# Down projections of a two-layer decoder: 20 of 43 blocks of K in Strassen quads with seven products for eight

## The chip, the core and the metric

The kernel runs on one core of a Trainium2 chip. The metric is the device time of one launch in microseconds. TensorE (PE) multiplies, with its weight loads (PEld) beside it; VectorE (DVE) and ScalarE (ACT) compute elementwise; GpSimd (POOL) and SyncE (SP) issue transfers here, and POOL does little else.

## The reference, cut to what matters

Two decoder layers on 256 tokens of width 2048. Layer 0 attends with 16 full heads, layer 1 with 16 query heads on 4 key-value heads, a sliding window and sinks. After each attention and each gated mixer the residual is normalised.

```
h = layer_norm(ALPHA * h + attn, ...)
ffn:  h @ w_up -> causal width-3 conv -> g, v = split;  (gelu(g) * v) @ w_down
h = layer_norm(ALPHA * h + ffn, ...)
```

`w_up` is 2048 x 11008, `w_down` 5504 x 2048 (43 blocks of 128 rows of K, four column chunks of 512). Everything is in float32.

## The kernel before

Every product of a float32 activation and a float32 weight is made of three matmuls in the format fp32r. Each operand is split in two: a rounded high part, by ScalarE's Copy, and a low part, the difference, by VectorE. A product is high x high, high x low and low x high. The weights come from one long stream in DRAM, `wst`, in the order of their use, in *halves* of 128 x 1024 floats (512 KB). `load_weights` (L75, issued by SP) brings a half into one of four `raw` buffers; `high_upto` (L94, ScalarE) and `low_piece` (L103, VectorE) split it into one of four pairs `wh`, `wl`. `take` asks for the half three ahead of the one that PE starts (`AHEAD`). When the low part of half s is made, its raw buffer is free and the load of half s+4 is issued. All engines run their instructions in the order in which the program records them; small work is recorded through an agenda: `at(n, f)` records `f` n slots later, where each half of the stream is one slot.

In the *up projection* (`ws_unit`, L244 and L246) the weights are stationary, a unit takes two halves, and VectorE does the convolution (L639 to L642), the gate (L645) and the split of the gated result (`store`, L650) into 43 blocks of `st` and `up`, where columns 0 to 255 are the high part of 256 tokens and columns 256 to 511 the low part.

In the *down projection* (`project_out`, with the class `Moving`, L307 to L309) the activations are stationary and 512 columns of weights move. A half holds two blocks of K for one chunk of 512 columns, and each block serves both token tiles: 12 matmuls a half. There are 43 x 4 blocks, so 86 halves a layer. Two PSUM banks hold a chunk; after it, `evac` adds them to the scaled residual `res` and takes the statistics (L380, L381). The last eight halves of the last chunk are the *window*: PE goes through them once for token tile 0 and a second time for tile 1, so that VectorE normalises tile 0 (L396, L397) and PE transposes it (L406) for the next stage during the second pass. The window's halves stay in places of their own (`aside`): in layer 0 in `xT` and in `st`. `settle` lets the splits run ahead there, in a ring of free places (`reach`), up to six halves into the next layer; VectorE has them all in order ahead of the evacuation of tile 0. Layer 1's end has only four places in `xT` and no ring.

`gb` holds the scale and bias of the norm (two transfers of 1 MB on POOL); `banks` of PSUM are four "acc" and four "at" tiles, and the down projection uses "acc" alone until its transposes.

Of the kernel before, what the change touches and what calls it, by code (L numbers as in the profile page):

```python
# [11 lines left out]
F32 = mybir.dt.float32  # L12
F32R = mybir.dt.float32r
AF = mybir.ActivationFunctionType
ALU = mybir.AluOpType
# [21 lines left out]
RAW_BUFS = 4  # L37
# [8 lines left out]
OPENING = 4  # L46


@with_exitstack
def trunk(ctx: ExitStack, tc: tile.TileContext, wst, xT_in, x_in, relb, onehot, umask, sinks, conv_in, ln_g, ln_b, out):  # L50
# [9 lines left out]
    gbp = ctx.enter_context(tc.tile_pool(name="gbp", bufs=1))  # L60

    n_halves = wst.shape[0]
# [7 lines left out]
    def load_weights(behind=None):  # L70
        u = todo["load"]
        if u < n_halves:
            raws[u] = wpool.tile([P, HW], F32, name="raw")
            for j, c in enumerate(pieces(u)):
                nc.sync.dma_start(raws[u][:, c], wst[u][:, c])  # L75
                if behind:
                    behind(j)
            todo["load"] += 1
# [70 lines left out]
    st = big.tile([P, NH, 2 * T], F32R, name="st")  # L149

# [197 lines left out]
    def project_out(src, nk, li, homes, preload, turnover=None):  # L348
# [4 lines left out]
        mv = Moving(src, nk)  # L353
        w0 = nexth["i"] + (nk * NCH - WINDOW_BLOCKS) // 2
        n0 = w0 + WINDOW
        after = homes is not None
        aside.update({w0 + j: (xT, j) for j in range(SPARE)})

        def settle():


            ring, h = homes()
            aside.update({w0 - len(ring) + j: x for j, x in enumerate(ring) if x})
            aside.update({w0 + SPARE + j: h[j] for j in range(4)})
            aside.update({n0 + 4: h[4], n0 + 5: h[5], n0 + 6: h[0], n0 + 7: h[1]})
# [8 lines left out]
        for i, a in enumerate((ln_g, ln_b)):  # L374
# [3 lines left out]
        def evac(n, t, acc):  # L378
            z = res[:, t, n * 512:(n + 1) * 512]
            nc.vector.scalar_tensor_tensor(z, z, ALPHA, acc, op0=ALU.mult, op1=ALU.add)  # L380
            nc.vector.bn_stats(stats[:, t, n, :], z)  # L381
# [33 lines left out]

        def late(t, i):
            last = i == WINDOW - 1
            if t == 0 and last:
                evac(NCH - 1, 0, accs[0])
                sd = moments(0)  # L420
                nc.vector.reciprocal(rs[0], sd)
                for c in COLS[0]:
                    norm(0, c)
            if t == 1 and after:
                if 3 <= i < 7:
                    c = COLS[0][i - 3]
                    low(0, c, turn(0, c))
                if 5 <= i < 7:
                    high_upto(n0 + i + 1)
            if t == 1 and last:  # L430
                evac(NCH - 1, 1, accs[1])
# [6 lines left out]
        for n in range(NCH):  # L438
            accs = [acc_tile(), acc_tile()]
            if n == 1 and turnover:  # L440
                turnover()
            if n == 1 and after:
                settle()
            if n < NCH - 1:
                mv.chunk(accs)
                for t in range(2):
                    at(0, evac, n, t, accs[t])
            else:
                nc.scalar.activation(junk, eps, AF.Sqrt)
                mv.chunk(accs, late=late)  # L450
# [65 lines left out]
    def layer_attention(l, rest, stage, turnover):  # L516
# [62 lines left out]

        if l == 0:  # L580
# [14 lines left out]
        return project_out(lambda k: oT[:, k, :], NH, 2 * l, turnover.homes, AF.Gelu_apprx_tanh, turnover)  # L595

    class FeedForward:
# [12 lines left out]
        def homes(self):  # L610
            x, h = ([(tile, j) for j in range(n)] for tile, n in ((xT, SPARE), (self.up, 6)))
            return x + h[:4] + HALF_BUFS * [None] + h[4:], h

        def block(self, k):
            return st[:, k, :] if k < NH else self.up[:, k - NH, :]

        def run(self, rest):
# [29 lines left out]
            def store(i, g):  # L647
                b = self.block(i)
# [22 lines left out]
            ws_opening(accs, between, opened)  # L671
            for u in range(OPENING, 2 * FT):
                acc = acc_tile()
                ws_unit(acc)
                after(u, acc)
            homes = None
            if l == 0:
                x, h = ([(tile, j) for j in range(n)] for tile, n in ((xT, SPARE), (st, 4)))
                homes = lambda: (x + HALF_BUFS * [None], h + [(self.up, j) for j in range(2)])
            return project_out(self.block, FT, 2 * l + 1, homes, AF.Exp)  # L680
# [41 lines left out]

def _stream(w_qkv, w_o0, w_kv, w_q, w_o1, w_up, w_down):
# [7 lines left out]
    def ffn(l):  # L731
        up = w_up[l]
        parts.append(np.stack([_still(up[:, :DFF]), _still(up[:, DFF:])], 1).reshape(-1, P, HW))
        parts.append(_moving(w_down[l]))
# [45 lines left out]
```

## Time and profile before

| what | value |
| --- | --- |
| median of 3 runs | 2093.8 us (2093.42 to 2095.63) |
| span of the profiled execution | 2091.8 us |
| TensorE busy | 2074.2 us (99%) |
| VectorE busy | 1439.6 us (69%) |
| ScalarE busy | 968.7 us (46%) |
| moved by the DMA engines | 405 MB, 194 GB/s in the mean |
| granted TensorE clock, mean | 0.998 |

For the profiled execution the span is given, from its first to its last instruction; it is 2.0 us under the median of the runs. In a row of a view by lines, the numbers after the bar are the busy time of the group, the mean length of one instruction in ns, and the idle time of the engine ahead of them with what ended it. In a timeline row, the first number is the start, the second the length, both in us; "[1.66 <-PE acc L309]" says that the engine stood idle for 1.66 us until that instruction was done. A matmul's length contains its passage through the array: the pace is read from the starts.

### The profile page before, as it was taken

The numbers are of one execution on the slowest core, as the hardware profiler recorded it, in microseconds if no ns is written. First come the engines' busy times: TensorE is split into PE (matmuls) and PEld (weight loads), VectorE is DVE, ScalarE is ACT, GpSimd is POOL, SyncE is SP. The second block draws the span as 40 slices with busy tenths as digits, with TensorE's granted clock in tenths as the row PEclk, the third lists the DMA queues.
The fourth block names the chain that finished last, engine by engine and source line by source line (L and its number), as shares of the span: only waits on it lengthen the run. The fifth ranks groups of instructions, "written<-read, shape, count | busy, mean of one in ns | idle before, by whom it ended". The sixth has DMA issues, their size and how long they took to land.

```text
span 2091.8 us, 28873 instructions
## 1 busy us (share of the span) xinstructions
PE 2074.2 (99%) x11076; PEld 1792.3 (86%) x11076; DVE 1439.6 (69%) x2106; ACT 968.7 (46%) x1397; POOL 23.5 (1%) x36
## 2 busy tenths in 40 slices
PE   9999999999999999999999999999999999999997
PEld 7888888988888888888888888898888888888886
DVE  5555567787877788744466676778778778765545
ACT  5444445344444454433353555444444454443342
POOL 0100000000000000000000000000000000000000
PEclk9999999999999999999999999999999999999999
DMA  8855557455555565655573745645556565566653
GB/s 273 305 167 180 166 181 253 161 173 191 185 192 188 190 189 185 205 197 192 191 261 125 248 149 186 232 152 191 182 195 188 186 194 185 191 202 196 195 192 131
DMA packets 114264, 405.09 MB, mean 194 GB/s; under 512 B 15648, under 2 KB 15968, under 8 KB 112848
## 3 DMA queue, kind: packets, MB, share of 16 engines
q1 hardware_dynamic: 106832, 383.67, 56.5%
q0 software_dynamic: 7008, 19.33, 2.6%
q8 instruction: 87, 1.43, 0.3%
q14 instruction: 49, 0.40, 0.1%
q10 hardware_dynamic: 288, 0.26, 0.1%
HBM read 401.02 MB, written 6.34 MB: 195 GB/s over the span
## 4 chain that ended last, share of the span: by engine, by line
PE 95%; DMA 2%; DVE 2%; ACT 1%; issue 0%; SPq 0%; ACTq 0%; DVEq 0%
PE acc L244 36%; PE acc L246 19%; PE acc L307 12%; PE acc L308 12%; PE acc L309 12%; DMA raw<-in_wst_dram 2%; PE acc L271 1%; PE at L499 1%; PE at L466 1%; ACT wh L94 1%; PE at L406 1%; DVE wl L103 0%; PE at L492 0%; PE at L465 0%; PE at L500 0%
## 5 line engine op out<-in xcount | busy, mean ns | idle before, releaser
L103 DVE TENSOR_TENSOR wl<-raw,wh 128x1024 fp32r<-128x1024 f32 (+1 forms) x663 | 790.8, 1220 | 303.8 <-ACT wh L94 297.9
L244 PE MATMUL acc<-xT,wh 128*128 128x512 f32 x3456 | 832.7, 392 | 0.0
L94 ACT ACTIVATE wh<-raw 128x1024 fp32r<-128x1024 f32 (+1 forms) x663 | 676.0, 1053 | 329.7 <-PE acc L309 272.2
L244 PEld LDWEIGHTS acc<-xT,wh 128*128 128x128 f32 x3456 | 641.1, 188 | 128.5
L246 PEld LDWEIGHTS acc<-xT,wl 128*128 128x128 f32 x3456 | 444.1, 190 | 14.9 <-DVE wl L103 2.4
L246 PE MATMUL acc<-xT,wl 128*128 128x256 f32 x3456 | 453.1, 284 | 1.8 <-DVE wl L103 1.8
L638 ACT ACTIVATE h<-acc 128x256 f32<-128x256 f32 x172 | 66.3, 385 | 411.3 <-PE acc L246 216.0
L639 DVE TENSOR_TENSOR h<-acc,h 128x256 f32<-128x256 f32 x172 | 73.0, 424 | 157.1 <-ACT h L638 157.1
L307 PE MATMUL acc<-wh,up 128*128 128x512 f32 x378 | 147.0, 389 | 0.0
L308 PE MATMUL acc<-wl,up 128*128 128x512 f32 x378 | 147.0, 389 | 0.0
L309 PE MATMUL acc<-wh,up 128*128 128x512 f32 x378 | 147.0, 389 | 0.0
L307 PE MATMUL acc<-wh,st 128*128 128x512 f32 x366 | 143.7, 393 | 0.0
L308 PE MATMUL acc<-wl,st 128*128 128x512 f32 x366 | 142.5, 389 | 0.0
L309 PE MATMUL acc<-wh,st 128*128 128x512 f32 x366 | 142.5, 389 | 0.0
L641 DVE SCALAR_TENSOR_TENSOR c<-h,cw,c 128x255 f32<-128x255 f32 x172 | 83.3, 484 | 6.1
L642 DVE SCALAR_TENSOR_TENSOR c<-h,cw,c 128x254 f32<-128x254 f32 x172 | 83.2, 484 | 6.2
L307 PEld LDWEIGHTS acc<-wh,up 128*128 128x128 f32 x378 | 70.9, 188 | 14.8
L309 PEld LDWEIGHTS acc<-wh,up 128*128 128x128 f32 x378 | 70.9, 188 | 14.8
L308 PEld LDWEIGHTS acc<-wl,up 128*128 128x128 f32 x378 | 71.0, 188 | 14.6
L309 PEld LDWEIGHTS acc<-wh,st 128*128 128x128 f32 x366 | 68.7, 188 | 14.5
L307 PEld LDWEIGHTS acc<-wh,st 128*128 128x128 f32 x366 | 68.7, 188 | 14.0
L308 PEld LDWEIGHTS acc<-wl,st 128*128 128x128 f32 x366 | 68.7, 188 | 13.9
(129 smaller groups left out, 1636.8 us busy)
## 6 DMA issues: line engine op xcount, KB each, us to landing
raw<-in_wst_dram SPq DMA_DIRECT2D x723, 512.0 KB, 4.2
band<-ud POOLq DMA_DIRECT2D x8, 512.0 KB, 13.4
bias<-band POOLq DMA_DIRECT2D x8, 512.0 KB, 6.3
gb<-in_ln_g_dram POOLq DMA_DIRECT2D x4, 1024.0 KB, 7.0
gb<-in_ln_b_dram POOLq DMA_DIRECT2D x4, 1024.0 KB, 10.1
res<-in_x_dram POOLq DMA_DIRECT2D x2, 1024.0 KB, 10.5
out_dram<-res SPq DMA_DIRECT2D x8, 256.0 KB, 2.5
xc<-in_xT_dram SPq DMA_DIRECT2D x7, 256.0 KB, 5.6
```

The source lines that it names most:

```text
L94: nc.scalar.activation(wh[:, c], raws[s][:, c], AF.Copy)
L103: nc.vector.tensor_tensor(out=wl[:, c], in0=raws[s][:, c], in1=wh[:, c].bitcast(F32), op=ALU.subtract)
L244: nc.tensor.matmul(acc, w, xT[:, k, :], start=(k == 0), stop=(k == ends[0]))
L246: nc.tensor.matmul(acc[:, 0:T], w, xT[:, k, 0:T], start=False, stop=(k == ends[1]))
L271: nc.tensor.matmul(part(accs[u]), cols(pair[u][k // 8][0], k % 8), part(xT[:, k, :]), start=(t == 0 and k == 0), stop=False)
L307: nc.tensor.matmul(acc, sh, wh, start=(k == 0), stop=False)
L308: nc.tensor.matmul(acc, sh, wl, start=False, stop=False)
L309: nc.tensor.matmul(acc, sl, wh, start=False, stop=(k == self.nk - 1))
L638: nc.scalar.activation(h, acc[:, T:2 * T], AF.Copy)
L639: nc.vector.tensor_tensor(out=h, in0=acc[:, 0:T], in1=h, op=ALU.add)
L641: nc.vector.scalar_tensor_tensor(c[:, 1:T], h[:, 0:T - 1], w[:, 1:2], c[:, 1:T], op0=ALU.mult, op1=ALU.add)
L642: nc.vector.scalar_tensor_tensor(c[:, 2:T], h[:, 0:T - 2], w[:, 0:1], c[:, 2:T], op0=ALU.mult, op1=ALU.add)
```

## The change

**Quads.** The first 20 blocks of K are taken as 10 quads: two blocks of K (k1, k2) by two token tiles (0, 1), times a pair of column chunks (n0, n1). The eight block products of a quad become seven (Winograd's form of Strassen), each of three matmuls: B11 and B21 with the blocks themselves, and five with a sum or difference on one side or both. Of the weights, `T1`, `T3`, `T2`, `T4` stand for sums and differences of B11, B12, B21, B22; of the activations, s1, s2, s4 are sums, and the difference of k1's two token tiles stands in the place of k1's second tile, written at the gate (`store`, for even i below 20). Two quads are a *run* of seven halves, in which a block of weights serves one product: 6 matmuls a half. The other 23 blocks stay plain, and their halves stand around the runs by `PLAINS`. The two column pairs have 58 halves each, 116 a layer for 86. All eight PSUM banks are used: four "acc", and four "at" for the sums P1, P5, P6, P7, which `fold` later adds to the residual.

**Weights.** The host puts B11, B12, B22, B21 of each quad into a second array `wsum`. `presums` loads them (two transfers of 512 KB on SP), lets VectorE form the four sums (1024 + 512 + 512 columns) and stores them to DRAM by POOL (1 MB), once for each of 20 quads and layer: four under attention, 16 in the up projection, one every nine slots. The runs load T halves from there. The buffer for it is the one of `gb`, so the down projection's two transfers into `gb` move to slots 54 and 103 of its 116.

**Activations.** `sums` and `split_sums` make s1, s2, s4 of two quads into `xT`, five times a layer, at the end of the run before.

**Rest.** The raw buffers become five. The places of layer 0's window are put in another order, since `st` and `xT` are read by quads until later. The scratch for DMA descriptors is set to 4096.

```diff
-RAW_BUFS = 4
+RAW_BUFS = 5
+NQ = 10
+PLAINS = ((5, 4, 3, 3, 3, 5), (2, 2, 2, 2, 2, 13))
+EARLY = 4
+SEVEN = (("B11", "B21"), ("T1", "T3"), ("T2", "T4"), ("B22", "B22"), ("B11", "B21"), ("T1", "T3"), ("T2", "T4"))
...
+    def presums(quads, first_slot, pitch):
+        area = gbp.tile([P, 2, D], F32, name="gb")
+        r, w = area[:, 0], area[:, 1]
+        def load(q, j):
+            js = slice(j * HW, (j + 1) * HW)
+            nc.sync.dma_start(r[:, js], wsum[q][:, js])
+        def first():
+            nc.vector.tensor_tensor(out=w[:, 0:HW], in0=r[:, 512:512 + HW], in1=r[:, 0:HW], op=ALU.subtract)
+        def second(q):
+            nc.vector.tensor_tensor(out=w[:, HW:HW + 512], in0=r[:, 0:512], in1=w[:, 512:HW], op=ALU.add)
+            nc.vector.tensor_tensor(out=w[:, HW + 512:], in0=r[:, HW + 512:], in1=w[:, HW:HW + 512], op=ALU.subtract)
+            nc.gpsimd.dma_start(wsums[q], w)
+        for i, q in enumerate(quads):
+            m = first_slot + pitch * i
+            at(m, load, q, 0)
+            at(m + 1, load, q, 1)
+            at(m + 5, first)
+            at(m + 6, second, q)
...
+            return [{"B11": (("P1", n), *token(k1, 0)), "B21": ((n0, 0), *token(k2, 0)), "T1": (("P5", n), *s1),
+                     "T3": (("P7", n), *token(k1, 1)), "T2": (("P6", n), *s2), "T4": ((n0, 1), *token(k2, 1)),
+                     "B22": ((n1, 0), *s4)}[b]]
...
+        def fold(c):
...
+            def first():
+                nc.scalar.activation(u, p1, AF.Copy)
+                into(0, n0, u)
+                nc.vector.tensor_tensor(out=u, in0=p6, in1=u, op=ALU.add)
+                nc.vector.tensor_tensor(out=v, in0=p5, in1=u, op=ALU.add)
+            def second():
+                into(0, n1, v)
+                nc.vector.tensor_tensor(out=u, in0=p7, in1=u, op=ALU.add)
+            def third():
+                into(1, n0, u)
+                into(1, n1, u)
+                into(1, n1, p5)
+            for i, f in enumerate((first, second, third)):
+                at(1 + i, f)
+        def sums(i):
...
+            nc.vector.tensor_tensor(out=g.rearrange("p (a b) -> p a b", a=4), in0=x[:, :, 0:T].bitcast(F32),
+                                    in1=x[:, :, T:2 * T].bitcast(F32), op=ALU.add)
...
+            for o, a, b, op in ((s2, gv[:, :, 1, 1], gv[:, :, 0, 1], ALU.subtract), (s1, s2, gv[:, :, 0, 0], ALU.add),
+                                (s4, gv[:, :, 1, 0], s2, ALU.subtract)):
+                nc.vector.tensor_tensor(out=o, in0=a, in1=b, op=op)
...
+        def split_sums(i, s):
+            hi, lo = (xsum(i)[:, h].rearrange("p s q c -> p (s q c)") for h in range(2))
+            nc.scalar.activation(hi, s, AF.Copy)
+            nc.vector.tensor_tensor(out=lo, in0=s, in1=hi.bitcast(F32), op=ALU.subtract)
...
+        if quads:
+            for i in range(NQ // 2):
+                at(1 + (i and sum(PLAINS[0][:i]) + 7 * (i - 1) + 2), all_sums, i)
...
+        presums([(l, *q) for q in QUAD_ORDER[:EARLY]], 4 if l else 40, 9)
...
             def store(i, g):
+                if i < 2 * NQ and i % 2 == 0:
+                    nc.vector.tensor_tensor(out=g[:, P:T], in0=g[:, 0:P], in1=g[:, P:T], op=ALU.subtract)
...
+            presums([(l, *q) for q in QUAD_ORDER[EARLY:]], 0, 9)
...
-    nc = _bacc.Bacc("TRN2", target_bir_lowering=False, num_devices=1)
+    nc = _bacc.Bacc("TRN2", target_bir_lowering=False, num_devices=1, dynamic_dma_scratch_size=4096)
```

On TensorE, before, in layer 0's down projection: two blocks of one half (`wh_8064`, `wl_8065`), each for both token tiles (banks `acc_8114` and `acc_8115`).

```order
L307 MATMUL acc_8114<-wh_8064,st_82 128x512
L308 MATMUL acc_8114<-wl_8065,st_82 128x512
L309 MATMUL acc_8114<-wh_8064,st_82 128x512
L307 MATMUL acc_8115<-wh_8064,st_82 128x512
L308 MATMUL acc_8115<-wl_8065,st_82 128x512
L309 MATMUL acc_8115<-wh_8064,st_82 128x512
```

Now, the end of the first run there: the T2 and T4 blocks of its last half (`wh_8444`, `wl_8445`), then the plain half behind it (`wh_8463`, `wl_8464`).

```order
L509 MATMUL at_8437<-wh_8444,xT_123 128x512
L510 MATMUL at_8437<-wl_8445,xT_123 128x512
L511 MATMUL at_8437<-wh_8444,xT_123 128x512
L509 MATMUL acc_8312<-wh_8444,st_125 128x512
L510 MATMUL acc_8312<-wl_8445,st_125 128x512
L511 MATMUL acc_8312<-wh_8444,st_125 128x512
L509 MATMUL acc_8308<-wh_8463,up_2986 128x512
L510 MATMUL acc_8308<-wl_8464,up_2986 128x512
```

Each block of the run has three matmuls for six, one product into one bank; the sums of activations come from `xT`.

On VectorE, at the same place, now: the splits of the run's last two halves (`wl_8432`, `wl_8445`), the sums of the next two quads, the split of the plain half, the low part of the sums. Before, splits alone stand in a row here.

```order
L168 TENSOR_TENSOR wl_8432<-raw_8352,wh_8431 128x1024
L168 TENSOR_TENSOR wl_8445<-raw_8372,wh_8444 128x1024
L564 TENSOR_TENSOR tmp_8450<-st_125 128x1024
L570 TENSOR_TENSOR tmp_8451<-tmp_8450 128x256
L570 TENSOR_TENSOR tmp_8451<-tmp_8451,tmp_8450 128x256
L570 TENSOR_TENSOR tmp_8451<-tmp_8450,tmp_8451 128x256
L168 TENSOR_TENSOR wl_8464<-raw_8390,wh_8463 128x1024
L576 TENSOR_TENSOR xT_123<-tmp_8451,xT_123 128x768
```

Four operations moved in between the split of the run's last half and that of the half behind it.

On VectorE at the end of layer 0's down projection, before: splits into `wl`, `xT`, `st` and `up` (the last six belong to the next layer), then the evacuation of tile 0.

```order
L103 TENSOR_TENSOR xT<-raw,xT 128x1024 x4
L103 TENSOR_TENSOR st<-raw,st 128x1024 x4
L103 TENSOR_TENSOR wl<-raw,wh 128x1024 x4
L103 TENSOR_TENSOR up<-raw,up 128x1024 x2
L380 SCALAR_TENSOR_TENSOR res<-res,acc 128x512
```

Now, from the splits of the window's fourth half on:

```order
L168 TENSOR_TENSOR st<-raw,st 128x1024 x2
L527 SCALAR_TENSOR_TENSOR res<-res,tmp 128x512
L550 TENSOR_TENSOR tmp<-at,tmp 128x512
L525 TENSOR_TENSOR res<-res,acc 128x512
L531 BN_STATS stats<-res 128x6
L527 SCALAR_TENSOR_TENSOR res<-res,acc 128x512
L168 TENSOR_TENSOR xT<-raw,xT 128x1024 x2
L525 TENSOR_TENSOR res<-res,tmp 128x512
L531 BN_STATS stats<-res 128x6
L527 SCALAR_TENSOR_TENSOR res<-res,tmp 128x512
L525 TENSOR_TENSOR res<-res,at 128x512
L168 TENSOR_TENSOR st<-raw,st 128x1024
```

Two parts of the fold (its first part, three operations, stands two splits and more ahead) and an evacuation moved in among the window's splits; behind these rows come the same six splits for the next layer and the evacuation of tile 0.

More of the change, by code (lines that the diff above doesn't have):

```diff
@@ L373, in project_out, with load_gb @@
         gb = gbp.tile([P, 2, D], F32, name="gb")
-        for i, a in enumerate((ln_g, ln_b)):
+        def load_gb(i):
+            a = (ln_g, ln_b)[i]
             nc.gpsimd.dma_start(gb[:, i], bass.AP(tensor=a.tensor, offset=a.offset + li * D, ap=[[0, P], [1, D]]))
-        ag, rs = {}, {}
[L378 to L381, printed above, removed]
+        whole = sum(PLAINS[0]) + 7 * (NQ // 2)
@@ new lines, in project_out, with product @@
+        for half in plan:
+            for e in half:
+                for key, _, _ in target(e):
+                    owed[key] = owed.get(key, 0) + 1
+        def product(key, sh, sl, wh, wl):
+            if key not in banks:
+                banks[key] = psum.tile([P, 512], F32, name="at" if key[0] in SUMS else "acc")
+                used[key] = 0
+            acc, first, last = banks[key], used[key] == 0, used[key] == owed[key] - 1
+            used[key] += 1
+            nc.tensor.matmul(acc, sh, wh, start=first, stop=False)
+            nc.tensor.matmul(acc, sh, wl, start=False, stop=False)
+            nc.tensor.matmul(acc, sl, wh, start=False, stop=last)
@@ new lines, in done, with zs, into @@
+        def done(*keys):
+            return all(used.get(key) == owed[key] for key in keys)
+        def zs(t, n):
+            return res[:, t, n * 512:(n + 1) * 512]
+        parts = {(t, n): 1 + (2 if (t, n % 2) == (1, 1) else 1) * quads for t in range(2) for n in range(NCH)}
+        scaled = set()
+        def into(t, n, a):
+            z = zs(t, n)
+            if (t, n) in scaled:
+                nc.vector.tensor_tensor(out=z, in0=z, in1=a, op=ALU.add)
+            else:
+                nc.vector.scalar_tensor_tensor(z, z, ALPHA, a, op0=ALU.mult, op1=ALU.add)
+                scaled.add((t, n))
+            parts[t, n] -= 1
+            if not parts[t, n]:
+                nc.vector.bn_stats(stats[:, t, n, :], z)
@@ new lines, in evac @@
+        def evac(n, t):
+            into(t, n, banks.pop((n, t)))
+        def fold(c):
+            n0, n1 = 2 * c, 2 * c + 1
+            p1, p5, p6, p7 = (banks.pop((b, c)) for b in SUMS)
+            w = tmpp.tile([P, HW], F32, name="tmp")
+            u, v = w[:, 0:512], w[:, 512:HW]
+            def first():
[12 more added lines that the diff above has]
+                at(1 + i, f)
@@ L414, in low, with window @@
                                     in1=xT[:, ks, t * P:(t + 1) * P].bitcast(F32), op=ALU.subtract)
+        def window(mv, halves):
+            blocks = []
+            for t in range(2):
+                for i, half in enumerate(halves):
+                    for j, e in enumerate(half):
+                        if t == 0:
+                            blocks.append(mv.block(min(AHEAD, WINDOW - 1 - i)))
+                        product(*target(e)[t], *blocks[2 * i + j])
+                    if t:
+                        step()
+                    late(t, i)
+                    if t:
+                        run(before)
         def late(t, i):
@@ L418, in late @@
             if t == 0 and last:
[L419 removed]
+                evac(NCH - 1, 0)
                 sd = moments(0)
```

159 lines of the change are left out of this document (129 added, 30 removed).

## The prediction

> **What bounds the kernel now.** I read the page first: how long the engines are busy, and what the chain that ended last is made of.
>
> ```profile
> span 2091.8 us, 28873 instructions
> ...
> PE 2074.2 (99%) x11076; PEld 1792.3 (86%) x11076; DVE 1439.6 (69%) x2106; ACT 968.7 (46%) x1397; POOL 23.5 (1%) x36
> ...
> PE 95%; DMA 2%; DVE 2%; ACT 1%; issue 0%; SPq 0%; ACTq 0%; DVEq 0%
> ```
>
> TensorE is the chain: 95% of it, busy 99% of the span. Then the stages, one row each: attention 0, up projection 0, down projection 0, down projection 1, and what follows the last matmul.
>
> ```profile
> core 0: us, PE busy (x) PEld busy (x) DVE busy (x) ACT busy (x) POOL busy (x), PEclk, DMA share, GB/s
> ...
> 30.00:390.00 360.00, 358.59 (x1879) 307.29 (x1879) 214.98 (x310) 169.00 (x265) 9.20 (x12) 1.00 0.63 207
> 390.00:874.00 484.00, 482.74 (x2829) 428.19 (x2828) 386.05 (x609) 232.19 (x348) 2.17 (x3) 1.00 0.58 186
> 874.00:1112.00 238.00, 238.00 (x1067) 197.41 (x1066) 131.23 (x126) 101.19 (x101) 0.00 (x0) 1.00 0.62 204
> ...
> 1842.00:2080.00 238.00, 238.00 (x1058) 197.09 (x1056) 123.25 (x118) 92.64 (x91) 0.00 (x0) 1.00 0.58 188
> 2080.00:2092.00 12.00, 0.04 (x1) 0.00 (x0) 7.45 (x12) 1.78 (x3) 0.00 (x0) 0.59 0.23 87
> ```
>
> Both down projections are TensorE without a gap, at full clock, with VectorE 55% and 52% busy: a matmul less is time less there, until a half comes late. The steady pace, from the timeline in down projection 0:
>
> ```profile
> 900.74 0.39 PE L309 MATMUL acc<-wh,up 128*128 128x512 f32 x1
> ...
> 900.96 0.39 PE L307 MATMUL acc<-wh,up 128*128 128x512 f32 x1
> ...
> 901.16 1.06 ACT L94 ACTIVATE wh<-raw 128x1024 fp32r<-128x1024 f32 x1 [1.66 <-PE acc L309]
> ...
> 902.26 1.23 DVE L103 TENSOR_TENSOR wl<-raw,wh 128x1024 fp32r<-128x1024 f32 x1 [1.49 <-ACT wh L94]
> ...
> 903.00 0.39 PE L307 MATMUL acc<-wh,up 128*128 128x512 f32 x1
> ...
> 904.36 0.39 PE L307 MATMUL acc<-wh,up 128*128 128x512 f32 x1
> ```
>
> Six matmuls start between 903.00 and 904.36: 0.227 us each, 2.72 us for a plain half (12 matmuls), 1.36 us for a half that serves one token tile (6). When PE is done with a half (0.96), ScalarE splits into the freed buffer at +0.20 and VectorE is done at +2.53.
>
> **What the change removes.** In each quad 7 products stand for 8; 2 layers x 2 column pairs x 10 quads x 3 matmuls = 120 matmuls less, and the order of instructions has exactly 120 fewer. 120 x 0.227 = **-27.2 us**, all on the path. Nothing else is removed; the price is that a quad's halves are used up in 1.36 us instead of 2.72, and everything that feeds them must follow.
>
> **Sums of activations, at the end of a run.** Seven quad halves form a run of 9.5 us. VectorE needs 1.22 of every 1.36 us for the splits. At the end of four of the five runs of the first column pair, the sums of the next run stand between the split of the run's last half and that of the plain half behind it.
>
> ```profile
> L103 DVE TENSOR_TENSOR wl<-raw,wh 128x1024 fp32r<-128x1024 f32 x661 | 789.4, 1222 | 299.5 <-ACT wh L94 293.7 <-issue 4.8
> ...
> L645 DVE TENSOR_TENSOR c<-c,c 128x256 f32<-128x256 f32 x86 | 36.6, 426 | 3.0
> ...
> L160 DVE TENSOR_TENSOR xT<-xc,xT 128x512 fp32r<-128x512 f32 x7 | 4.8, 686 | 0.6 <-ACT xT L159 0.6
> ```
>
> One addition of 1.22 and three of 0.43 us are 2.5. The last quad half's split is done 2.53 us after PE frees its buffer, the sums at 5.0, the next split at 6.2; PE, four halves ahead, wants that low part at 4 x 1.36 + 0.23 = 5.67. A stall of 0.6, eight times: **+4.8 us** (0 if VectorE runs a little ahead, 8 if waits between the four operations add 0.4 each time). The split of the sums (768 columns, between the rows of 512 and 1024: 0.95) follows under a plain half and is hidden; so are the fold and the evacuations between the column pairs, since five plain halves (13.6 us) and two more hold them.
>
> **Loads in the runs.** The first column pair needs ten halves in 7 x 1.36 + 3 x 2.72 = 17.7 us (1.77 each), the second nine in 15.0 (1.66 each), and a run by itself 1.36, which is 385 GB/s. The hardest loading before is the ring ahead of the window, at the end of down projection 0:
>
> ```profile
> 1055.72 0.68 DVE L380 SCALAR_TENSOR_TENSOR res<-res,acc 128x512 f32<-128x512 f32 x1
> ...
> 1058.36 1.21 DVE L103 TENSOR_TENSOR wl<-raw,wh 128x1024 fp32r<-128x1024 f32 x1
> 1059.49 3.49 DVE L103 TENSOR_TENSOR xT<-raw,xT 128x1024 fp32r<-128x1024 f32 x3
> ...
> 1077.48 1.23 DVE L103 TENSOR_TENSOR xT<-raw,xT 128x1024 fp32r<-128x1024 f32 x1 [0.62 <-ACT xT L94]
> ...
> 1096.99 1.23 DVE L103 TENSOR_TENSOR up<-raw,up 128x1024 fp32r<-128x1024 f32 x1 [0.23 <-ACT up L94]
> 1099.72 0.69 DVE L380 SCALAR_TENSOR_TENSOR res<-res,acc 128x512 f32<-128x512 f32 x1 [1.50 <-PE acc L309]
> ...
> 1103.03 0.75 DVE L397 SCALAR_TENSOR_TENSOR res<-res,rs,gb 128x512 f32<-128x512 f32 x1
> ```
>
> And the times from issue to landing of that line's loads between 1070 and 1080:
>
> ```profile
> DMA to landing us min/median/max: 4.5/4.7/5.7
> ```
>
> Between 1077.48 and 1096.99 eleven more halves follow, 1.77 us apart, each landing 4.7 us after its issue. That pace is four raw buffers' own: (4.7 + 2.3 for the two splits) / 4 = 1.76. Five at the same landing would give 1.4. What the memory can do:
>
> ```profile
> 5.00:10.00 5.00, 4.51 (x16) 2.92 (x14) 3.11 (x6) 3.55 (x7) 0.00 (x0) 1.00 0.98 374
> 80.00:90.00 10.00, 8.59 (x39) 6.74 (x38) 5.86 (x10) 4.84 (x10) 1.64 (x3) 1.00 0.91 303
> ...
> 1075.00:1080.00 5.00, 5.00 (x23) 4.14 (x23) 3.39 (x3) 3.70 (x4) 0.00 (x0) 1.00 0.92 309
> ```
>
> 374 GB/s is 1.40 us a half, 309 is 1.70. At 1.77 only the second pair is short: 9 x 1.77 - 14.96 = 1.0, ten times, 9.9 us; at 1.66 or less nothing, since up to eight halves stand loaded or split when a run begins. I take 1.6 with **+1.5 us** for single late ones. The Trainium skill, DMA: Bandwidth & Descriptors, section Bandwidth, speaks against runs at such a pace: 1 MB transfers measured 341 GB/s, which is an estimated 1.54 us a half, slower than 1.36. By it each run alone would fall behind, but not a whole group; the sum by it has 0 here, by the ring's row 9.9.
>
> **End of layer 0.** VectorE there works, in order, through 22 splits (the last 16 of the projection, 6 of the next layer), the second fold and an evacuation (12 operations on 512 columns), and only then evacuates the first token tile. From 1055.72 to 1058.36 four such operations took 2.64 us, 0.66 each; three splits took 3.49. So 22 x 1.14 + 12 x 0.67 = 33.1 us; it starts 1.2 us into the last run: 34.3. PE needs 6 x 1.36 + 5 x 2.72 + 8 x 1.36 = 32.6 to the end of its first pass through the window. Before, the 22 splits filled 1059.49 to 1098.22, 38.7 us, and VectorE then still waited 1.5 us for PE. Now with loads at 1.6 and the second scale vector's 1 MB among them I put VectorE's end near 39. The norm's first quarter comes 4.06 us behind the evacuation (1099.72 to 1103.78), PE wants its transposes four halves of the second pass, 5.5 us, behind the first: 39 + 4.06 - 38.1 = 5.0, and half a microsecond for late splits in the pass: **+5.5 us** (0.3 if VectorE never idles; 9.3 at the old loading pace with the 1 MB, 43.3). The Trainium skill, TensorE: Matmul & The Clock Gate, Part 1, has a rule that would add to it: after an idle window of about 3.4 us the clock halves, for about as long. Here 1.4 us idle in 80 to 90 left it at 1.00, and 12 us at the end brought 0.59; by the rule the sum would be an estimated 1.7 us longer.
>
> **End of layer 1.** No ring. From PE's end with the first half of the last five plain ones: split of 107 at 2.5, fold's first part 4.7, 108 at 5.9, second part and evacuation 9.6, 109 at 10.8, third part 13.7, 110 at 15.0; PE wants 110 at 4 x 2.72 + 2 x 1.36 + 0.23 = 13.8: **+1.1 us** (0 to 2.5).
>
> **Sums of weights.** 40 of them, each 1.22 + 2 x 0.69 = 2.6 us of VectorE, two loads on SP, one store on POOL. Under attention (VectorE 60% busy) they are hidden. In the up projection:
>
> ```profile
> 605.69 2.35 DVE L103 TENSOR_TENSOR wl<-raw,wh 128x1024 fp32r<-128x1024 f32 x2
> 609.39 0.42 DVE L639 TENSOR_TENSOR h<-acc,h 128x256 f32<-128x256 f32 x1 [1.35 <-ACT h L638]
> ...
> 615.01 0.42 DVE L639 TENSOR_TENSOR h<-acc,h 128x256 f32<-128x256 f32 x1 [0.64 <-ACT h L638]
> ...
> 616.84 2.36 DVE L103 TENSOR_TENSOR wl<-raw,wh 128x1024 fp32r<-128x1024 f32 x2
> ```
>
> ```profile
> 609.01 2.08 PE L246 MATMUL acc<-xT,wl 128*128 128x256 f32 x16
> ```
>
> VectorE idles 1.35 + 0.64 = 2.0 us in the 11.15 of two units, 4.5 us in the nine slots of one sum, and the low halves are 2 us early (the first done at 606.9, wanted at 609.01). I count one late 0.8 a layer, where both parts and the gate's difference meet: **+1 us** (0 to 5). The weights' queues: 186 GB/s at 0.58 is 320 at 1.0, and 2.1 MB in 25 us add 84: a share of 0.84. No DMA of these waits for work that is late, so SP's weight loads behind them go on.
>
> **The sum.** -27.2 + 4.8 + 1.5 + 5.5 + 1.1 + 1 = -13.3; 2091.8 becomes 2078.5. The runs shown have a median of 2093.8, 2.0 above the span, so **2080.5 us**. The terms' ends give 2066.9 and 2101.3.
>
> **Rivals.** (1) *The cover holds*: VectorE gets ahead in the plain halves, the sums cost nothing and the layer ends 3: 2093.8 - 27.2 + 3 = 2069.6. For: VectorE was 55% busy; against: the splits can't pass the four buffers that PE frees. Chance 0.17. (2) *Loads keep the ring's 1.77*: + 9.9 for 1.5, and the layer end 9.3 for 5.5: 2092.7, no change. For: the only row of a long burst; against: that had four raw buffers. 0.10. (3) *Slower*: loads reach 1.9 in the runs, because quads, sums and stores share the engines: ten groups of each kind (10 x 1.9 - 17.68 and 9 x 1.9 - 14.96) give 34.6 for 1.5: 2113.6. It decides from 1.80 on, where its stalls (14.8 us) eat the gain that is left. For: 303 GB/s in 80 to 90, where POOL moved too, is 1.73; against: POOL moves little in the down projection. 0.06. (4) *VectorE bounds the up projection*: 32 sums at 0.5 us each, 16 for 1: 2095.5. It has 2.0 us per 11.15 against it. 0.06. That fewer matmuls leave the time alone can't be: no wait stands in either stage.
>
> **Numbers.** The forecast has 0.61 (its own range 2073 to 2088), the rivals 0.17, 0.10, 0.06, 0.06. A measurement of this kernel tells 0.2% (4.2 us) from no change: below 2089.6 is faster. Forecast, cover and a fifth of (2) make 0.80 faster; the rest of (2) and most of (4) 0.13 the same; 0.07 slower. The range 2068 to 2093 holds nearly all of the forecast, most of rival 1 and half of 2, and leaves out 3 and most of 4.
>
> **What would show it.** 120 fewer matmuls; eight gaps of some 0.6 us on TensorE behind runs, released by the split's VectorE line; one of 4 to 5 us at the transposes that end layer 0; loads landing in 5 us or so within the runs. Gaps inside the runs, released by the load, would speak for 2 or 3; gaps in the up projection for 4; none at all for 1.

## The result, and the profile after

The changed kernel takes **2077.5 us** in the median of 4 runs (2077.01 to 2079.92), the kernel before 2094.5 in the same session (2093.42 to 2095.63): a ratio of 0.9922, 95% interval 0.9908 to 0.9936. That is 17 us less, 3 below the 2080.5 that were forecast. The profiled execution has a span of 2076.0 us for 2091.8. The page after: busy times, and the chain by engine.

```profile
span 2076.0 us, 29434 instructions
...
PE 2051.3 (99%) x10956; PEld 1769.7 (85%) x10956; DVE 1654.0 (80%) x2388; ACT 1037.2 (50%) x1471; POOL 46.5 (2%) x76
...
PE 90%; DVE 6%; DMA 2%; ACT 1%; issue 1%; SPq 0%; DVEq 0%; ACTq 0%
```

TensorE has 120 matmuls fewer and VectorE 214 us more work; VectorE now holds 6% of the chain, where it had 2%. The same stages as before, by windows (the down projections are shorter):

```profile
30.00:390.00 360.00, 360.00 (x1889) 308.86 (x1889) 224.41 (x323) 170.40 (x267) 11.34 (x16) 1.00 0.68 231
390.00:874.00 484.00, 482.50 (x2826) 427.65 (x2825) 425.23 (x667) 230.42 (x347) 11.55 (x19) 1.00 0.74 256
874.00:1100.00 226.00, 220.30 (x970) 181.07 (x969) 185.64 (x190) 132.69 (x132) 0.00 (x0) 0.99 0.83 284
1828.00:2064.00 236.00, 234.83 (x1054) 193.81 (x1052) 190.18 (x201) 132.23 (x134) 0.00 (x0) 1.00 0.76 261
```

Attention 0 lost its gap (358.59 busy before, 360.00 now), VectorE is 82% busy in down projection 0, and there alone the mean clock is under 1.00. Both traces hold every matmul, and TensorE's order differs only within the down projections; so the time of the same matmul in both says in which stage the difference arises:

| stage | layer 0 | layer 1 |
| --- | --- | --- |
| attention | -1.9 us | 0.0 |
| up projection | +0.8 | +1.5 |
| down projection, to the next stage (layer 1: to 20 us before the end) | -5.1 | -11.1 |

Each down projection should have lost 13.6 us; layer 0 gave 8.5 of that back, layer 1 gave 2.5. Two kinds of gap hold this. The first, behind a run, on VectorE's timeline (L564 and L570 make the sums of activations, L168 is the split):

```profile
893.05 2.58 DVE L168 TENSOR_TENSOR wl<-raw,wh 128x1024 fp32r<-128x1024 f32 x2
895.55 1.22 DVE L564 TENSOR_TENSOR tmp<-st 128x1024 f32<-128x1024 f32 x1
896.80 1.22 DVE L570 TENSOR_TENSOR tmp<-tmp 128x256 f32<-128x256 f32 x3
897.93 1.22 DVE L168 TENSOR_TENSOR wl<-raw,wh 128x1024 fp32r<-128x1024 f32 x1
```

2.4 us of sums part the split of the run's last half from the next one, which is done at 899.15. TensorE's timeline at the same place:

```profile
898.55 0.39 PE L509 MATMUL acc<-wh,up 128*128 128x512 f32 x1
899.21 0.50 PE L510 MATMUL acc<-wl,up 128*128 128x512 f32 x1 [0.27 <-DVE wl L168]
```

It wanted the low part at 898.78, 0.23 after its matmul at 898.55, and begins at 899.21. That happens eight times: TensorE starts 0.43 late, and the matmul behind comes another 0.11 late. The second kind, on TensorE's timeline at the end of layer 0:

```profile
1092.39 0.39 PE L511 MATMUL acc<-st,up 128*128 128x512 f32 x1
1097.39 1.12 PE L605 MATMUL at<-ident,res 128*128 128x128 f32 x4 [4.62 <-DVE res L596]
1098.16 0.78 PE L509 MATMUL acc<-st,up 128*128 128x512 f32 x1
1098.73 0.63 PE L510 MATMUL acc<-st,up 128*128 128x512 f32 x1
1099.16 0.63 PE L511 MATMUL acc<-st,up 128*128 128x512 f32 x1
1099.59 0.63 PE L509 MATMUL acc<-st,up 128*128 128x512 f32 x1
```

TensorE waits 4.62 us for the norm, and then its matmuls start 0.43 us apart where they were 0.227: half clock.

### The profile page after: what moved, and what is told of

Its sections match the earlier page's. It is cut to its first block, busy times and chain, and to the rows that moved or that the text cites. A ratio compares the mean times of both kernels' runs of the same rounds, so it can differ in the third digit from the quotient of the medians.

```text
span 2076.0 us, 29434 instructions
## 1 busy us (share of the span) xinstructions
PE 2051.3 (99%) x10956; PEld 1769.7 (85%) x10956; DVE 1654.0 (80%) x2388; ACT 1037.2 (50%) x1471; POOL 46.5 (2%) x76
## 4 chain that ended last, share of the span: by engine, by line
PE 90%; DVE 6%; DMA 2%; ACT 1%; issue 1%; SPq 0%; DVEq 0%; ACTq 0%
PE acc L313 37%; PE acc L315 19%; PE acc L510 7%; PE acc L511 7%; PE acc L509 7%; DVE wl L168 2%; PE acc L377 2%; PE acc L376 2%; PE acc L378 2%; PE acc L340 1%; PE at L511 1%; PE at L509 1%; PE at L510 1%; DMA raw<-in_wst_dram 1%; ACT wh L159 1%; DMA raw<-ws 1%
## 5 line engine op out<-in xcount | busy, mean ns | idle before, releaser
L168 DVE TENSOR_TENSOR wl<-raw,wh 128x1024 fp32r<-128x1024 f32 (+1 forms) x723 | 860.7, 1219 | 165.2 <-ACT wh L159 150.8
L159 ACT ACTIVATE wh<-raw 128x1024 fp32r<-128x1024 f32 (+1 forms) x723 | 737.9, 1053 | 225.8 <-PE acc L511 102.5
L510 PE MATMUL acc<-wl,up 128*128 128x512 f32 x330 | 129.3, 392 | 2.3 <-DVE wl L168 2.3
L511 PE MATMUL acc<-wh,up 128*128 128x512 f32 x330 | 128.5, 389 | 0.0
L509 PE MATMUL acc<-wh,up 128*128 128x512 f32 x330 | 128.5, 389 | 0.0
L871 DVE TENSOR_SCALAR c<-h,cw 128x256 f32<-128x256 f32 x172 | 71.0, 413 | 6.2
L509 PEld LDWEIGHTS acc<-wh,up 128*128 128x128 f32 x330 | 62.0, 188 | 12.9
L509 PE MATMUL acc<-wh,st 128*128 128x512 f32 x184 | 72.8, 396 | 0.0
L511 PEld LDWEIGHTS acc<-wh,up 128*128 128x128 f32 x330 | 61.9, 188 | 12.7
L511 PE MATMUL acc<-wh,st 128*128 128x512 f32 x184 | 71.7, 390 | 0.0
L510 PE MATMUL acc<-wl,st 128*128 128x512 f32 x184 | 71.7, 389 | 0.0
L376 PE MATMUL acc<-wh,xT 128*128 128x512 f32 x144 | 58.2, 404 | 1.0 <-ACT wh L159 0.6
L800 ACT ACTIVATE qT<-acc 128x256 f32<-128x256 f32 x32 | 12.3, 384 | 90.8 <-PE acc L315 66.3
## 6 DMA issues: line engine op xcount, KB each, us to landing
band<-ud POOLq DMA_DIRECT2D x8, 512.0 KB, 13.6
```

What stands on the lines that cost most here:

```text
L159: nc.scalar.activation(wh[:, c], raws[s][:, c], AF.Copy)
L168: nc.vector.tensor_tensor(out=wl[:, c], in0=raws[s][:, c], in1=wh[:, c].bitcast(F32), op=ALU.subtract)
L376: nc.tensor.matmul(acc, sh, wh, start=(k == 0), stop=False)
L509: nc.tensor.matmul(acc, sh, wh, start=first, stop=False)
L510: nc.tensor.matmul(acc, sh, wl, start=False, stop=False)
L511: nc.tensor.matmul(acc, sl, wh, start=False, stop=last)
```

## The experiments

Every ratio is to the kernel before in the same session; the changed kernel's is 0.9922. Stage times come from the same matmul in two traces, so the 1.8 us that some launches lose in their first 30 us drop out. The intervals of experiments 1, 2, 4 and 8 overlap that of the changed kernel, so their ratios alone settle nothing; what is said of them rests on the stage times of one trace each.

**1. The sums one half later.**

```diff
-at(1 + (i and sum(PLAINS[0][:i]) + 7 * (i - 1) + 2), all_sums, i)
+at(1 + (i and sum(PLAINS[0][:i]) + 7 * (i - 1) + 3), all_sums, i)
```

> The additions that make the second to fifth set of sums of activations are recorded one half later, behind the split of the first plain half after the run. Theory (their place costs: 2.5 us of VectorE between the split of a run's last half, which is late, and the split that PE wants next): the eight stalls of 0.54 us behind the runs vanish, none takes their place, because the next split is then wanted 2.72 us later; the span falls by 4.4 us, from 2076.0 to 2071.6. Rival (VectorE is simply full in a run and behind it, 1.2 of 1.36 us, so that 2.5 us more are late wherever they stand): the eight stalls stay at 0.4 us or more, now one plain half later, and the span stays within 1 us of 2076.0.

Ratio 0.9907 (0.9892 to 0.9923). All eight gaps are gone; one of 0.67 us has come a half behind the last of layer 0. The first pair of layer 0 is 1.5 us shorter, that of layer 1 2.2. VectorE's timeline at the same run, which stands 1.7 us later in this launch:

```profile
894.72 3.95 DVE L168 TENSOR_TENSOR wl<-raw,wh 128x1024 fp32r<-128x1024 f32 x3
898.58 1.22 DVE L564 TENSOR_TENSOR tmp<-st 128x1024 f32<-128x1024 f32 x1
899.84 1.22 DVE L570 TENSOR_TENSOR tmp<-tmp 128x256 f32<-128x256 f32 x3
900.97 1.22 DVE L168 TENSOR_TENSOR wl<-raw,wh 128x1024 fp32r<-128x1024 f32 x1
```

The sums now stand behind three splits, and the split behind them may take 2.72 us longer. It was their place, not a full engine. The span of the profiled launch fell by 1.0 us only, not by 4.4: it lost 1.9 in its first 30 us, and layer 0's end took 1.0 longer, since two windows of 3.413 us ran at half clock there instead of one.

**2. The second fold's last part behind the norm, in layer 0.**

```diff
-at(1 + i, f)
+at(6 if f is third and c and after else 1 + i, f)
```

> In layer 0 the third part of the second fold (three additions into the residual of token tile 1 and one bn_stats, 2.6 us of VectorE by 4 x 0.66) is recorded behind the norm of token tile 0 instead of ahead of its evacuation. Theory (VectorE's queue ahead of the evacuation sets the stall at the transposes): the stall of 4.6 us shrinks by 2.6 to 2.0; and as 2.0 us are under an idle window that halves the clock, the 3.4 us at half clock behind it go too (1.5 us): together -4.1, a span of 2071.9. Rival A (the loads set when the splits ahead of the evacuation are done, so the queue behind them closes up and the evacuation comes no sooner): the stall stays at 4.6, span 2076. Rival B (the half clock does not come from the idle time): the stall shrinks to 2.0 and the 3.4 us at half clock stay, span 2073.4.

Ratio 0.9917 (0.9899 to 0.9935). The stall shrank by 2.0 us, to 2.65, and the half clock stayed; the windows, on the grid of 3.413 us in which the clock is recorded:

```profile
1093.97:1097.38 3.41, 0.76 (x6) 0.34 (x5) 2.94 (x7) 0.29 (x1) 0.00 (x0) 1.00 0.81 288
1097.38:1100.80 3.42, 3.42 (x13) 2.73 (x12) 3.31 (x6) 0.60 (x1) 0.00 (x0) 0.50 0.02 5
```

So VectorE's queue does set the stall. The 0.6 us short of 2.6 is VectorE idling for the last splits, up to 1.01 us at a time. And 2.65 us idle suffice to halve the clock.

**3. Four raw buffers.**

```diff
-RAW_BUFS = 5
+RAW_BUFS = 4
```

> Four raw buffers in place of five, nothing else. Theory (a load is asked for when its buffer's split is done, so the pace of the loads is landing and two splits by the number of buffers: (4.7 + 2.3) / 4 = 1.76 us a half, and five give 1.4): the second column pair's groups of nine halves, used up in 15.0 us, fall behind by up to 0.9 each, ten of them; with 3 us of lead at each pair's start this gives stalls of some 3 to 8 us in the runs, released by the loads or by splits that waited for them; the stall at 84 us in attention 0 comes back with 1.7; at layer 0's end the splits ahead of the evacuation come later by up to 22 x 0.3 and the stall there grows by 2 to 4. Together 2076 + 7 to 14. Rival (the plain halves and the split buffers give all the lead that is needed): no stall in the runs, at most the 1.7 of attention 0: 2077.7.

Ratio **1.0117** (1.0101 to 1.0133), median 2118.6: slower than the kernel before. The mechanism is the one expected; the size, 41 us, is three times the upper end of the 7 to 14 expected. Its chain by engine, from the page:

```profile
PE 75%; DMA 11%; DVE 10%; ACT 3%; issue 1%; ACTq 0%; SPq 0%; DVEq 0%
```

DMA holds 11% of the chain for 2%. Against the changed kernel down projection 0 is 19.7 us longer, down projection 1 20.1, and the stall of attention 0 is back with 1.1. By the starts of the same matmuls, the loss is not spread evenly:

| us longer than the changed kernel | layer 0 | layer 1 |
| --- | --- | --- |
| five runs of the first column pair, with the plain halves between them | 5.0 | 6.0 |
| five runs of the second, the same | 9.7 | 10.2 |
| first pass through the window (eight halves, 6 matmuls each) | 2.4 | 4.0 |
| from there to the next stage | 2.6 | 0.0 |

A run of the second pair, with two plain halves ahead of it, loses 2.0 us in the mean; one of the first pair, with three to five, loses 1.0 to 1.2.

**4. Sums of weights eight slots later in the up projection.**

```diff
-presums([(l, *q) for q in QUAD_ORDER[EARLY:]], 0, 9)
+presums([(l, *q) for q in QUAD_ORDER[EARLY:]], 8, 9)
```

> In the up projections the sixteen sums of weights begin eight slots later, so that each stands at the same place among the units (same parity, same position against the gate). Theory (the first sum comes when VectorE has not yet caught up behind the opening): the stalls of 0.84 us and 0.28 of pipeline at 440 and 1406 us go and none takes their place: -2.2, a span of 2073.8. Rival (this sum stands in the one phase of nine where both parts and the gate's difference meet ahead of a low half): the same two stalls come back four units (22 us) later, span 2076.

Ratio 0.9917 (0.9901 to 0.9932). The stalls at 440 and 1406 are gone, and smaller ones, 0.47 us, stand 22 to 23 us later, at 462 and 1429. Each theory is borne out in part: a stall comes back four units later, as the rival had it, but less than half as large as the 1.1 us lost right behind the opening.

**5. The kernel before with five raw buffers.**

```diff
-RAW_BUFS = 4
+RAW_BUFS = 5
...
-nc = _bacc.Bacc("TRN2", target_bir_lowering=False, num_devices=1)
+nc = _bacc.Bacc("TRN2", target_bir_lowering=False, num_devices=1, dynamic_dma_scratch_size=4096)
```

> The kernel before with five raw buffers and the smaller descriptor scratch that makes room for them; no quads. Theory (the stall of before at 84 us in attention 0, 1.9 us in all, is a load that four buffers ask for too late, and nothing else before waits for loads): the stall goes, the span falls by 1.9 to 2089.9; in the ring ahead of layer 0's window the splits then follow each other at (4.7 + 2.3) / 5 = 1.4 us instead of 1.77, which shortens nothing, since PE is not waiting there. Rival (the stall went for the changed order of attention 0 with the sums of weights, not for the buffer): 2091.8, and the ring's splits stay 1.7 us apart if that pace is the memory's.

Ratio 0.9987 (0.9977 to 0.9996), span 2089.2: 1.85 us less in attention 0, as in the changed kernel, and 0.76 in up projection 0. VectorE's timeline in the ring:

```profile
1076.45 1.23 DVE L103 TENSOR_TENSOR xT<-raw,xT 128x1024 fp32r<-128x1024 f32 x1 [1.49 <-ACT xT L94]
1077.59 4.62 DVE L103 TENSOR_TENSOR st<-raw,st 128x1024 fp32r<-128x1024 f32 x4
1083.52 2.49 DVE L103 TENSOR_TENSOR wl<-raw,wh 128x1024 fp32r<-128x1024 f32 x2 [1.30 <-ACT wh L94]
1086.73 2.44 DVE L103 TENSOR_TENSOR wl<-raw,wh 128x1024 fp32r<-128x1024 f32 x2 [0.72 <-ACT wh L94]
1089.10 2.53 DVE L103 TENSOR_TENSOR up<-raw,up 128x1024 fp32r<-128x1024 f32 x2
```

From the split at 1076.45 to the last, which starts 1.27 after 1089.10, ten more follow, 1.39 us apart where four buffers made 1.77. The pace of the ring was the buffers', as the prediction had it, and the gap in attention 0 came of having only four.

**6. Without the sums.** Both calls of `presums` and that of `all_sums` are left out, and `source.append(taken - 1 - j)` stands in the place of the T halves' source: they read once more a block that the stream read a few loads before.

> The changed kernel without all that makes sums: neither the sums of weights (their halves are read from the stream instead, so these products use other blocks) nor the sums of activations are made; quads, runs, folds and loads stay. Theory (120 matmuls are worth 27.2 us on the path, and the sums cost the eight stalls, 4.4 us, and the two in the up projections, 2.2): span 2076.0 - 6.6 = 2069.4, with 6.3 us left at layer 0's end. Rival (the sums of weights, 80 MB of loads and stores, cost more than their two stalls, because they slow the weight loads of the attention and up projection): under 2066, or gaps gone where the theory has none. Rival 2 (the quads' stalls come from the pace of the runs and not from the sums): the eight gaps stay, 2073.8.

Ratio 0.9895 (0.988 to 0.991), span 2068.3, against the changed kernel 7.7 us less: 4.7 where the eight gaps were, 2.2 in the up projections, 0.8 at layer 0's end. Without the sums down projection 1 is 13.5 us shorter than before the change: 60 matmuls by 0.227 are 13.6, all of it on the path. Neither rival shows: nothing else got faster.

**7. 35 quad halves in a row.**

```diff
-PLAINS = ((5, 4, 3, 3, 3, 5), (2, 2, 2, 2, 2, 13))
+PLAINS = ((5, 4, 3, 3, 3, 5), (10, 0, 0, 0, 0, 13))
```

> In the second column pair the plain halves stand 10 ahead of the runs and 13 behind them, none between: 35 quad halves in a row, 47.6 us, twice. Theory (loads are paced by five buffers: landing 5.2 + two splits 2.3, by five = 1.50 us a half against 1.36 that PE takes; a lead of some 3 us when the runs start): 35 x 0.14 - 3 = 1.9 us of stalls a layer, span 2079.8. Rival A (what the DMA engines and the memory give is 1.7 a half, 309 GB/s, and plain halves between runs were the cover): 35 x 0.34 - 3 = 8.9 a layer, released by loads, span 2093.8. Rival B (nothing limits the runs, single halves at 1.36 can be had for as long as one likes): no stall, 2076.0.

Ratio 0.9996 (0.9987 to 1.0006): the whole gain is gone. The second pairs lose 9.0 us in layer 0 and 6.7 in layer 1 (6.9 and 6.1 in the row, the rest in the first pass through the window behind it), close to rival A's 8.9. Where its loads come from and land, in the 42 us of runs of layer 0:

```profile
DMA packets 3697, 13.49 MB, mean 321 GB/s; under 512 B 410, under 2 KB 410, under 8 KB 3693
...
raw<-ws SPq DMA_DIRECT2D x13, 512.0 KB, 6.0
raw<-in_wst_dram SPq DMA_DIRECT2D x12, 512.0 KB, 6.0
```

321 GB/s are 1.63 us a half. The plain halves between the runs are needed. Rival A's reason, the memory, is not proved by that: (6.0 + 2.3) / 5 is 1.66, so five buffers with slower landings give the same. Experiments 10 and 11 part them.

**8. Transposes that fill the stall.** Fourteen `nc.tensor.transpose(pt[:, 0:P], ident, ident)` ahead of the first of `turn(0, ...)` in layer 0.

> In layer 0, fourteen transposes of the identity stand on TensorE ahead of the first real transposes at the window's end, where PE idles 4.6 us for the norm; their result is overwritten. By 4 transposes in 1.12 us they take 3.9 us, less than the wait. Theory (the 3.4 us at half clock behind the stall come from PE's idle time): PE is idle for some 0.8 us only, the half clock is gone, and the matmuls behind run at 0.227 at once: -1.5 us, span 2074.5. Rival (the half clock comes with the work behind the stall, or from a wait of any kind): it stays, span 2076.

Ratio 0.9922 (0.9907 to 0.9936), span 2075.3: nothing won. The filler was too short. TensorE's timeline:

```profile
1092.38 1.69 PE L606 MATMUL at<-ident 128*128 128x128 f32 x14
1096.60 0.85 PE L608 MATMUL at<-ident,res 128*128 128x128 f32 x4 [2.52 <-DVE res L596]
```

At full clock fourteen take 1.69 us (I had scaled a row that ran at half clock), 2.52 us stayed idle, and the next window stood at 0.50. That says what experiment 2 said, and nothing on the filling.

**9. Three places put right at once.** The sums as in 1; `presums(..., 1, 8)`; and in layer 0 the two last splits for the next layer behind the norm:

```diff
-reach[i] = min(max(reach[i], w0 + s), n0 + 5)
+reach[i] = min(max(reach[i], w0 + s), n0 + (3 if quads else 5))
...
                 for c in COLS[0]:
                     norm(0, c)
+                if quads and after:
+                    split_upto(n0 + 5)
```

> Three changes of place in the changed kernel. (a) The sums of activations one half later, as tried alone. (b) In the up projections the sums of weights begin one slot later and stand every eight slots in place of nine, so that none is at the place against the gate that stalled. (c) At the end of layer 0 VectorE makes the last two of the six splits for the next layer behind the norm of token tile 0, and not ahead of its evacuation; the fold stays where it is. Theory: (a) 3.7 us less, as when it was tried alone, (b) 2.2, (c) in the changed kernel VectorE was done with the last split but two at 91.3 us where PE ended its first pass at 92.4 (1000 us left out), so the evacuation then waits for PE alone, the norm's first quarter is done 4.1 us behind, before PE wants it, 5.4 us behind: the stall of 4.8 us goes, and with no idle time there is no half clock, 1.5 us more. Together -12.2: a span of 2063.8. Rival: the two splits moved are late for the next layer's opening, and the stall of (c) comes back there with 2 to 5 us: 2066 to 2069; rival to the clock: 3.4 us at half clock stay without any idle time, +1.5.

Median **2067.3 us**, ratio **0.9869** (0.9852 to 0.9885), the fastest of all. From 30 us on the launch is 11.6 us shorter than the changed kernel: 2.3 in the up projections, 3.7 for the sums (a gap of 0.63 is left), 5.6 at layer 0's end. Its windows there:

```profile
1088.50:1091.91 3.41, 3.41 (x16) 2.64 (x15) 2.95 (x7) 1.41 (x3) 0.00 (x0) 1.00 0.94 344
1091.91:1095.32 3.41, 3.01 (x18) 2.41 (x18) 3.34 (x6) 1.61 (x3) 0.00 (x0) 1.00 0.47 190
1095.32:1098.73 3.41, 3.41 (x20) 2.84 (x19) 3.38 (x5) 1.92 (x3) 0.00 (x0) 1.00 0.00 0
```

0.40 us idle, and no half clock. One sentence of the expectation was wrong: 92.4 is where TensorE reaches the transposes; its first pass ends four halves earlier, at 87.2. So VectorE is still late after the move, by what is left of the stall (0.40), and no split comes late in the next layer.

**10. Loads by themselves.** A loop over 64 halves for each number of buffers; in the last four parts each half is split as in the kernel. One run; TensorE does nothing in it, so each row begins with VectorE.

> A kernel that computes nothing of the reference: it only loads halves of the stream (512 KB each), 64 in each of ten parts, with 2, 3, 4, 5, 6 and 8 buffers that are free again as soon as 8 columns are copied, and then with 4, 5, 6 and 8 buffers that are free when ScalarE and VectorE have split the half (the two splits take 2.3 us). Theory (a load costs some 1.4 us of the DMA engines and lands a fixed time after its issue, so the number of buffers sets the pace until the engines are full): without splits the pace falls from 2 to 4 buffers and stays at 1.4 us from 4 or 5 on, 374 GB/s; with splits 4 buffers give 1.75 to 1.87, 5 give 1.4 to 1.5, 6 and 8 are at 1.4. Rival (what the memory gives for long is 1.6 to 1.7 us a half, as in the 35 quad halves in a row, whatever the buffers): 8 buffers without splits are not under 1.6, and with splits 5, 6 and 8 all stand at 1.6 to 1.7.

GB/s is the last column; the rows are 2, 3, 4, 5, 6, 8 buffers without splits, then 4, 5, 6, 8 with them.

```profile
10.00:140.00 130.00, 9.80 (x57) 0.00 (x0) 0.00 (x0) 1.00 0.74 234
150.00:250.00 100.00, 10.14 (x59) 0.00 (x0) 0.00 (x0) 1.00 0.90 307
260.00:340.00 80.00, 10.14 (x59) 0.00 (x0) 0.00 (x0) 1.00 1.00 389
350.00:420.00 70.00, 9.27 (x54) 0.00 (x0) 0.00 (x0) 1.00 1.03 408
435.00:505.00 70.00, 9.11 (x53) 0.00 (x0) 0.00 (x0) 1.00 1.03 409
520.00:590.00 70.00, 9.10 (x53) 0.00 (x0) 0.00 (x0) 1.00 1.03 408
605.00:710.00 105.00, 70.80 (x58) 63.24 (x60) 0.00 (x0) 1.00 0.86 294
725.00:810.00 85.00, 68.00 (x57) 58.48 (x56) 0.00 (x0) 1.00 0.96 345
825.00:900.00 75.00, 69.90 (x58) 61.30 (x58) 0.00 (x0) 1.00 1.03 409
915.00:985.00 70.00, 65.66 (x55) 57.02 (x54) 0.00 (x0) 1.00 1.03 410
```

A half is 524,288 bytes: 409 GB/s is 1.28 us, less than the 1.36 that a quad half lasts. With splits, four buffers give 1.78, five 1.52, six 1.28. The rival (1.6 to 1.7 whatever the buffers) has fallen: up to 409 GB/s the buffers set the pace, not the memory. That is shown for loads alone, with no other transfers beside them.

**11. The row of 35 again, all from the stream.** Experiment 7 with experiment 6's source for the T halves; the sums are still made and stored.

> The 35 quad halves in a row once more, with one difference: the T halves are read from the stream (other blocks, so the products that should take the sums of weights do not) and not from the array in which the sums were stored, whose rows are twice as long. The sums are still made and stored. Theory (five buffers give landing and two splits by five; loads from the stored sums land later, which made 5.6 to 6.0 of the 5.3 that five buffers with splits showed by themselves): the loads in the row land after 5.2 to 5.3 us, 1.50 us a half, and the stalls of the second column pair fall from 8.6 and 6.6 us to some 2 to 3 a layer. Rival (the landing is long because PE frees the split buffers in bursts, so loads are asked for in bursts, whatever their source): landings of 5.6 to 6.0 and 6 to 9 us a layer stay.

One run, span 2084.7. The loads of layer 0's runs:

```profile
raw<-in_wst_dram SPq DMA_DIRECT2D x27, 512.0 KB, 5.2
```

27 loads in 42 us where experiment 7 had 25, landing after 5.2 us for 6.0, and the second pairs lose 4.1 us each for 9.0 and 6.7. That is more than the 2 to 3 expected; 2.8 and 3.6 of it are lost in the row, the rest in the first pass through the window. Some half of experiment 7's loss thus goes with the source; the pace of five buffers, (5.2 + 2.3) / 5 = 1.50, makes the other half. What in the source does it is open. The stored sums have rows twice as long and lie elsewhere, and here the T halves read again what was read a few loads before; neither was tried by itself. Nor do loads of the stored sums always land later than the stream's: 6.0 for both in layer 0 of experiment 7, 5.9 against 5.2 in its layer 1, 4.3 against 4.9 in the second pair of layer 0 of experiment 3.

## Why the prediction was right, point by point

| term | forecast | measured | by |
| --- | --- | --- | --- |
| 120 matmuls | -27.2 | -27.1 | layer 1 without sums, -13.5, twice |
| sums of activations | +4.8 | +4.7 | experiment 6 |
| late loads in the runs | +1.5 | 0 | no gap there |
| end of layer 0 | +5.5 | +6.2 | experiment 9: 5.6 won, 0.56 left |
| end of layer 1 | +1.1 | 0.1 | one gap |
| sums of weights | +1 | +2.2 | experiment 6 |
| the fifth buffer | not in the sum | -2.6 | experiment 5 |
| sum | -13.3 | -16.5 | the two spans: -15.8 |

The 0.7 us between the last two stand at the openings of the up projections: the stall there is 1.09 in layer 1, where it was 0.68 before, and 1.00 in layer 0, where experiment 5 left 0.66. What makes these two longer was not tried. The sum came nearer than its terms: the loads, layer 1's end and the buffer are 5.1 us below the forecast, the rest some 2.6 above it, so that the time is right within 3 us in part by luck.

**The gain** is as forecast: TensorE had no gap, and 0.227 us a matmul came off the path. **The sums of activations** stalled eight times for the reason given, their place in VectorE's queue; experiment 1 moved them and the gaps went. **The end of layer 0** was VectorE's queue: I had put the evacuation at 39 us, and it started at 1093.64, 39.0 after the point from which I counted (the end of the first pass, 1087.2, less 32.6). The half microsecond for late splits did not come; the half clock that I left out of the sum did, and experiment 9 puts 1.4 us on it. The Trainium skill's rule (TensorE: Matmul & The Clock Gate, Part 1) that I weighed gave an estimated 1.7 and was right in kind; its idle window of about 3.4 us was not needed, 2.65 did it (experiment 2). **The end of layer 1**: VectorE began the fold earlier than I had it, since splits had run ahead; the gap is 0.07. **The sums of weights** make one gap in each up projection, as counted, of 0.84 and 0.28 behind it, not 0.5. **The fifth buffer's own gain** I had left out although the row that shows it (8.59 of 10 us busy in 80 to 90) stood in the prediction as a rate of the memory: it was a late request.

**The loads** are the term that came right for a reason I had half wrong. I compared whole groups, nine halves at the loads' pace with 15.0 us, so that 1.6 a half cost nothing, and 1.80 was where it decides. The runs show that a run must be held against itself. Seven halves at pace p fall behind by 7 x (p - 1.36), and only a lead gathered in the plain halves ahead of them makes up for it. Experiment 3 gives the lead. At 1.78 a run falls behind by 2.9; 2.0 are lost where two plain halves stand ahead of it, 1.0 to 1.2 where three to five do, so the lead is some 0.9 us or 1.8. A likely reason, not tested by itself, is that loads cannot run further ahead in plain halves than buffers stand free. At 1.50 to 1.52 a run falls behind by 1.0 to 1.1, which is just covered: no gap is there. 35 halves at 1.50, with ten plain ones ahead, give 4.9 - 1.8 = 3.1, where experiment 11 lost 2.8 and 3.6 in the row. By this estimate, 1.6 would have cost some 0.8 us in each of the ten runs of the second pairs, 8 us and half of the gain; counting the window's first pass too, the gain would have gone near 1.65. Rival 2's and rival 3's prices were too low, and the pace that decides is not 1.80: the changed kernel stands, by the estimate, little more than a tenth of a microsecond a half from it, and with one raw buffer less, at 1.78, it is slower than the kernel before. The 341 GB/s for 1 MB that I set against the runs (the Trainium skill, DMA: Bandwidth & Descriptors, section Bandwidth) is not the limit of such a stream here: with five buffers experiment 10 kept up 409 GB/s.

## What to carry to other kernels

When a bound engine gets less to do, look at who must now deliver faster, and hold each burst against the pace of its supplier by itself: an average with the slack between bursts only holds as far as buffers can store the lead. The pace of a stream is landing plus the time in use, by the number of buffers, until the DMA engines are full (409 GB/s here); one buffer was worth 41 us of 2077, more than the change itself. Small work on a second engine costs by its place in the queue: 3.7 us went by recording it one half later, 5.6 by letting two splits pass behind a norm.

## What the runs showed of the hardware

The clock is decided in windows of 3.413 us on a fixed grid: in the changed kernel the half clock at layer 0's end lasts 3.413 us, and the full clock behind it 965.97, which is 283 times that. About half a window of idle time can be enough to halve the clock for the next one. Over the twelve traces of the kernels (idle time from the matmuls' starts and modelled ends), every window at full clock in which TensorE idled 1.80 us or more, 2.08, 2.52, 2.65 and 3.24 among them, was followed by a window at 0.50, and every one with 1.59 or less by one at 1.00. Between them it went both ways: 0.50 behind 1.64 and 1.75, 1.00 behind 1.65, 1.73 and 1.76 (experiments 4, 7 and 3). What decides there is open. One that kept the full clock, from experiment 4: the first window is busy for 1.76 us of 3.42, which leaves some 1.65 idle, and the second still has 1.00.

```profile
1091.05:1094.47 3.42, 1.76 (x8) 1.13 (x6) 2.21 (x3) 1.06 (x1) 0.00 (x0) 1.00 0.99 367
1094.47:1097.88 3.41, 0.21 (x2) 0.21 (x3) 2.95 (x7) 0.29 (x1) 0.00 (x0) 1.00 0.93 335
```

So a stall of 2.65 us cost as much in clock as one of 4.62, one window at half clock, and one of 0.40 cost nothing more.
